# All SBUF tiles of a hybrid decoder step moved by 32 bytes

## Chip, cores and metric

The kernel runs on one core of one Trainium2 chip. The metric is the device time in microseconds (us) of one execution. Before the change it is 1095.63 us, the median of 3 runs (1095.52 to 1095.88).

## What is computed

One inference step of a hybrid decoder layer, in fp32, for a prompt group (512 tokens) and a sample group (8 sequences of 8 tokens). Both share the weights, so the kernel treats them as one block of 576 tokens with 1024 features. Cut to what matters:

```
x = x + post(Wout[concat(Mamba2-SSD heads, mLSTM heads)](pre(x)))   # one combined input projection
x = x + post(CrossAttn(pre(x), memory K/V))
x = x + post((silu(u @ w_gate) * (u @ w_up)) @ w_down),  u = pre(x)  # SwiGLU
```

Every bracket is an RMSNorm, a set of dense projections and some work by head or by token. The projections are nearly all of the work on TensorE.

## The kernel before

**Split products.** A projection is not multiplied in plain fp32. Weights and activations are each split into two fp32r tiles, a rounded copy `hi` and the rest `lo = raw - hi`, and a product is the sum of three matmuls into the same PSUM tile. This is `gemm`, lines 194 to 205, whose three matmuls are lines 201, 202 and 204:

```
mm(ps, wh, ah, start=i == 0, stop=False)
mm(ps, wh, al, start=False, stop=False)
m = mm(ps, tiles[order[c]][1], xh(order[c], t0, n), start=False, stop=c == len(tiles) - 1)
```

`wh` and the third matmul's weight are 128x128 blocks of tiles `whi` and `wlo`; they are the stationary operand, which TensorE loads first (rows PEld). `ah` and `al` are the moving operand, 256, 320 or 288 tokens wide (`HALVES` and `EHALVES`, lines 29 and 32). Lines 1848 to 1850 are the same three matmuls in the feed-forward part, and line 814 those of the mLSTM values, 512 columns wide, where the weights are the moving operand and the activations the stationary one. In all, 6,976 matmuls have fp32r operands: 2,176 with 256 columns, 2,784 with 288, 1,696 with 320, 288 with 512 and 32 with 258.

**Where the parts come from.** `split_w` (line 171) loads 512 KB of weights into a tile `raw`, ScalarE (ACT) casts it to `whi` (line 179), and VectorE (DVE, line 186) or GpSimd (POOL) subtracts. For some tiles a DMA that adds makes `wlo` instead (line 184). `whi` and `wlo` have three buffers each, `raw` has two. Activations are split in the same way (`split`, line 189).

**Order.** The build runs with a scheduler that places instructions by a simulated timeline; the later stages are recorded in an order written out by hand. Each engine then has one fixed list of instructions, with semaphores between them.

**Memory.** All tiles come from pools. The pools of one kind are stacked upward from the bottom of SBUF: `const` (line 120), `weights` (121), `big` (122, the activation slots `s0`, `s1` and so on), `ml` (278) and the pools that come and go above them. The pools with `side="right"` (lines 680, 940, 1034, 1101, 1380, 2047, 2088) are stacked downward from the top end of SBUF. Inside a pool each tile is rounded up to a multiple of 32 bytes. The pool `const` begins with two long-lived tiles:

```
c32 = cp.tile([P, NLONG], F32, name="c32")
par = cp.tile([P, NPAR], F32, name="par")
```

`c32` has 141 columns (564 bytes a partition, rounded to 576) and `par`, the gains and biases by feature, has 150 (600 bytes, rounded to 608). In the built program `c32` begins at byte 16,512 of a partition, `par` at 17,088, and the next tile at 17,696, which is 276 times 64 plus 32. All tiles behind it have sizes that are multiples of 64 bytes or come in groups that are, so that nearly every operand of a split product begins 32 bytes past a multiple of 64.

Of the kernel before, what the change touches and what calls it, by code (L numbers as in the profile page):

```python
# [11 lines left out]
F32 = mybir.dt.float32  # L12
# [7 lines left out]
P = 128  # L20
# [30 lines left out]
NPAR = _n  # L51
# [64 lines left out]
def build(nc, tc, ctx, I, O):  # L116
    V, A, G, S, TE = nc.vector, nc.scalar, nc.gpsimd, nc.sync, nc.tensor
    mm = TE.matmul

    cp = ctx.enter_context(tc.tile_pool(name="const", bufs=1))  # L120
    wp = ctx.enter_context(tc.tile_pool(name="weights", bufs=1))
    big = ctx.enter_context(tc.tile_pool(name="big", bufs=1))
    pg = ctx.enter_context(tc.tile_pool(name="pg", bufs=3, space=PSUM))
# [25 lines left out]


    c32 = cp.tile([P, NLONG], F32, name="c32")
    par = cp.tile([P, NPAR], F32, name="par")

    def C32(k):
        a, b = _c32[k]
# [144 lines left out]
    psw = MP("ps_warm")  # L300
    for _ in range(NWARM):
        mm(psw[:, 0:256], wz[:, 0:128], wz, start=True, stop=True, skip_group_check=True)
    S.dma_start(par, I["par"])

    wi = [[wp.tile([P, 1024], F32R, name=k, tag=k, bufs=3) for k in ("whi", "wlo")] for _ in range(2)]
    raws = [wp.tile([P, 1024], F32, name="raw", tag="raw", bufs=2) for _ in range(2)]
# [2049 lines left out]
```

## Time and profile before

| what | before |
|---|---|
| median of 3 runs | 1095.63 us |
| span of the profiled execution | 1095.0 us |
| TensorE matmul rows (PE), busy | 1084.1 us, 99% |
| TensorE weight loads (PEld), busy | 1027.5 us, 94% |
| VectorE (DVE) busy | 754.0 us, 69% |
| ScalarE (ACT) busy | 611.7 us, 56% |
| GpSimd (POOL) busy | 225.8 us, 21% |
| mean granted TensorE clock | 0.998 |
| DMA | 182.29 MB, mean 166 GB/s |

The span is that of one profiled execution, from its first instruction to its last; the median of the runs lies 0.6 us above it. The profile gives every instruction a start and a duration. Matmuls overlap each other in the array: a row's duration (0.28 us for 256 columns, say) is longer than the distance from its start to the next one's start (0.12 us). What a matmul costs in a stream is therefore read from the starts in the timeline and not from the durations. L201 is line 201 of the kernel.

### The profile page before, as it was taken

What the parts mean: (1) busy time and instruction counts of PE and PEld (TensorE: products, weight loads), DVE (VectorE), ACT (ScalarE), POOL (GpSimd) and SP (SyncE); (2) the same over time, 40 slices, a digit from 0 to 9 for tenths busy, and PEclk for the clock granted to TensorE, in tenths of its full rate; (3) what the DMA queues carried; (4) which work ended last, traced back from release to release, by engine and by line L of the source; (5) the groups of instructions that cost most, each with busy time, mean ns of one, the idle gap of its engine ahead of it and who ended that gap; (6) DMA issues with size and microseconds to landing.
All of it is one profiled execution on the core that took longest, in us unless ns stands there. A gap on an engine that the chain in (4) does not pass through costs nothing.

```text
span 1095.0 us, 20715 instructions
## 1 busy us (share of the span) xinstructions
PE 1084.1 (99%) x8124; PEld 1027.5 (94%) x8124; DVE 754.0 (69%) x1507; ACT 611.7 (56%) x1098; POOL 225.8 (21%) x305
## 2 busy tenths in 40 slices
PE   9999999999999999999999999999999999999997
PEld 8999887778999999999988879999999999999997
DVE  6896785658877775558744546676566877787555
ACT  7767632455654555656545445645566566656653
POOL 1332643313213112000144301100011121111000
PEclk9999999999999999999999999999999999999999
DMA  6785635435655349653467775644386687588532
GB/s 204 170 154 127 170 111 174 163 84 177 189 149 146 106 132 312 205 189 102 150 215 271 264 248 163 217 161 109 104 195 142 150 196 173 116 188 186 128 130 88
DMA packets 58967, 182.29 MB, mean 166 GB/s; under 512 B 6605, under 2 KB 11853, under 8 KB 58357
## 3 DMA queue, kind: packets, MB, share of 16 engines
q1 hardware_dynamic: 42740, 138.06, 39.0%
q0 software_dynamic: 15552, 41.95, 19.8%
q8 instruction: 64, 1.05, 0.4%
q10 hardware_dynamic: 576, 0.95, 0.3%
q14 instruction: 35, 0.28, 0.1%
HBM read 160.28 MB, written 20.65 MB: 165 GB/s over the span
## 4 chain that ended last, share of the span: by engine, by line
PE 88%; DVE 5%; ACT 4%; DMA 2%; issue 1%; SPq 0%; POOL 0%; DVEq 0%; ACTq 0%
PE ps_v L814 5%; PE ps_in L202 4%; PE ps_in L201 4%; PE ps_in L204 4%; PE ps_o L202 3%; PE ps_o L204 3%; PE ps_o L201 3%; PE ps_g L1848 3%; PE ps_g L1849 3%; PE ps_g L1850 3%; PE ps_u L1848 3%; PE ps_u L1850 3%; PE ps_u L1849 3%; PE ps_dn L1848 2%; PE ps_dn L1849 2%; PE ps_dn L202 2%
## 5 line engine op out<-in xcount | busy, mean ns | idle before, releaser
L201 PE MATMUL ps_in<-uh,whi 128*128 128x320 f32 (+1 forms) x544 | 164.0, 302 | 0.4 <-DVE cb L450 0.4
L204 PE MATMUL ps_in<-uh,wlo 128*128 128x320 f32 (+1 forms) x544 | 163.2, 300 | 0.0
L202 PE MATMUL ps_in<-ul,whi 128*128 128x320 f32 (+1 forms) x544 | 162.7, 299 | 0.0
L179 ACT CAST whi<-raw 128x1024 fp32r<-128x1024 f32 (+1 forms) x104 | 105.2, 1013 | 96.2 <-PE ps_in L202 26.1
L186 DVE TENSOR_TENSOR wlo<-raw,whi 128x512 fp32r<-128x512 f32 (+1 forms) x96 | 96.6, 1009 | 66.5 <-ACT whi L179 65.8
L201 PEld LDWEIGHTS ps_in<-uh,whi 128*128 128x128 f32 x544 | 103.1, 190 | 3.4 <-issue 1.7
L204 PEld LDWEIGHTS ps_in<-uh,wlo 128*128 128x128 f32 x544 | 103.0, 190 | 1.2 <-issue 0.4
L202 PEld LDWEIGHTS ps_in<-ul,whi 128*128 128x128 f32 x544 | 103.1, 190 | 0.6
L184 POOL DMA_DIRECT2D wlo<-win x32 | 27.9, 871 | 80.1 <-ACT wlo L183 72.0
L1848 PE MATMUL ps_g<-b,whi 128*128 128x288 f32 x144 | 42.5, 295 | 0.0
L1849 PE MATMUL ps_g<-b,whi 128*128 128x288 f32 x144 | 42.4, 295 | 0.0
L1848 PE MATMUL ps_u<-b,whi 128*128 128x288 f32 x144 | 42.4, 295 | 0.0
L1849 PE MATMUL ps_u<-b,whi 128*128 128x288 f32 x144 | 42.4, 295 | 0.0
L1821 ACT CAST whi<-rawx 128x1024 fp32r<-128x1024 f32 (+1 forms) x26 | 25.7, 987 | 27.8 <-PE ps_dn L1849 13.8
L191 DVE TENSOR_TENSOR wlo<-sw,whi 128x1024 fp32r<-128x1024 f32 (+1 forms) x26 | 29.6, 1140 | 14.9 <-ACT whi L190 14.7
L201 PE MATMUL ps_xo<-qh,whi 128*128 128x288 f32 x128 | 38.5, 302 | 0.2 <-ACT whi L179 0.2
L202 PE MATMUL ps_o<-mixs_l,whi 128*128 128x320 f32 (+1 forms) x128 | 38.2, 299 | 0.0
L204 PE MATMUL ps_o<-mixm_h,wlo 128*128 128x256 f32 (+1 forms) x128 | 38.2, 298 | 0.0
L202 PE MATMUL ps_o<-mixm_l,whi 128*128 128x256 f32 (+1 forms) x128 | 37.9, 296 | 0.0
L201 PE MATMUL ps_xq<-u2h,whi 128*128 128x320 f32 (+1 forms) x128 | 37.9, 300 | 0.0
L201 PE MATMUL ps_o<-mixm_h,whi 128*128 128x256 f32 (+1 forms) x128 | 37.9, 296 | 0.0
L204 PE MATMUL ps_xq<-u2h,wlo 128*128 128x320 f32 (+1 forms) x128 | 37.9, 296 | 0.0
(765 smaller groups left out, 3838.9 us busy)
## 6 DMA issues: line engine op xcount, KB each, us to landing
raw<-win SPq DMA_DIRECT2D x35, 512.0 KB, 3.9
raw<-wout SPq DMA_DIRECT2D x17, 512.0 KB, 3.6
raw<-wxq SPq DMA_DIRECT2D x13, 512.0 KB, 3.6
raw<-wgate SPq DMA_DIRECT2D x13, 512.0 KB, 3.5
raw<-wup SPq DMA_DIRECT2D x13, 512.0 KB, 5.3
wlo<-win POOLq DMA_DIRECT2D x24, 256.0 KB, 5.1
kva<-kc SPq DMA_DIRECT2D x12, 512.0 KB, 5.7
kva<-vc SPq DMA_DIRECT2D x12, 512.0 KB, 6.0
```

Of the source, the lines that this page charges most:

```text
L179: casts.append(A.copy(hi[:, :n], raw[:, :n]))
L184: G.dma_start(lo[:, a:b], src[:, a:b], accum_op=ALU.add)
L186: e.tensor_tensor(lo[:, a:b], raw[:, a:b], hi[:, a:b].bitcast(F32), op=ALU.subtract)
L191: (eng or V).tensor_tensor(lo, src, hi.bitcast(F32), op=ALU.subtract)
L201: mm(ps, wh, ah, start=i == 0, stop=False)
L202: mm(ps, wh, al, start=False, stop=False)
L204: m = mm(ps, tiles[order[c]][1], xh(order[c], t0, n), start=False, stop=c == len(tiles) - 1)
L814: mm(ps, a, b, skip_group_check=True, **kw)
L1821: A.copy(s.h3[:, s.all], s.r2[:, s.all])
L1848: mm(ps, wh, b[0][k], start=start and k == 0, stop=False, skip_group_check=True)
L1849: mm(ps, wh, b[1][k], start=False, stop=False, skip_group_check=True)
L1850: m = mm(ps, wl, b[0][k], start=False, stop=k == nk - 1, skip_group_check=True)
```

## The change

```
+    edge = ctx.enter_context(tc.tile_pool(name="edge", bufs=1, side="right"))
+    edge.tile([P, 8], F32, name="edge")
...
-    par = cp.tile([P, NPAR], F32, name="par")
+    par = cp.tile([P, 160], F32, name="par")
...
-    S.dma_start(par, I["par"])
+    S.dma_start(par[:, 0:NPAR], I["par"])
```

`par` becomes 640 bytes a partition in place of 608, so the tile behind it begins at 17,728, which is 277 times 64, and everything that is stacked upward lies 32 bytes higher than before. The tile `edge` (8 columns, 32 bytes) is never read or written; it takes the topmost 32 bytes, so everything that is stacked downward lies 32 bytes lower. `par` is filled by the same DMA with the same 150 columns. Nothing else is different. Instruction for instruction, the lists of all five engines are the same in the two built programs, with the same semaphores; only the addresses are others. 957 tiles lie 32 bytes higher, 153 lie 32 bytes lower.

Of the 6,976 fp32r matmuls, 6,944 had both operands at 32 past a multiple of 64, and have both at a multiple of 64 now. The other 32 (line 987) had their stationary operand at a multiple of 64 and have it at 32 past now.

Two relations change or stay, beside the plain position. Between two tiles of the same stack the distance is as before. Between a tile of the lower stack and one of the upper stack it changes by 64 bytes. Take the moving operand of a matmul and the stationary operand of the next one, which is loaded while the first one streams: in 5,434 such pairs the two stood a multiple of 128 bytes apart, and still do; in 1,275 they stood 64 bytes off a multiple of 128, and now are a multiple of 128 apart.

## The prediction

> **What bounds the kernel now.** The page comes first: busy shares, the granted clock, and the chain that ended last.
>
> ```profile
> span 1095.0 us, 20715 instructions
> PE 1084.1 (99%) x8124; PEld 1027.5 (94%) x8124; DVE 754.0 (69%) x1507; ACT 611.7 (56%) x1098; POOL 225.8 (21%) x305
> PEclk9999999999999999999999999999999999999999
> PE 88%; DVE 5%; ACT 4%; DMA 2%; issue 1%; SPq 0%; POOL 0%; DVEq 0%; ACTq 0%
> ```
>
> TensorE holds 88% of the chain, at full clock throughout. The list of waits shows nearly nothing that it waits for; these are its two longest:
>
> ```profile
> PE ps_warm L302 <- DVE wz L299: 1.1, 1, 1.1
> PE ps_ss L227 <- DVE ssqx L268: 0.8, 1, 0.8
> ```
>
> Where is the chain not on TensorE? In the first 112 us, by the chain for that window alone:
>
> ```profile
> by line: DVE ac L462 13.7%; issue 9.0%; DMA xraw<-xT 8.2%; DMA raw<-win 7.5%; ACT whi L179 6.5%; DVE cb L450 5.3%; ACT ac L460 5.2%; DVE pl L500 5.1%; DVE ssqx L268 3.4%; DVE wlo L186 2.8%; ACT wlo L183 2.6%; ACT L464 2.3%; DVE mrw L520 1.2
> ```
>
> DVE, ACT and the first loads set the pace there. Behind that, TensorE does. The table by stage (length, then busy us and instructions of PE, PEld, DVE, ACT, POOL, then clock, DMA share and GB/s) shows the room that the others have:
>
> ```profile
> 60.00:112.00 52.00, 51.15 (x374) 49.26 (x374) 41.39 (x76) 38.84 (x64) 17.82 (x44) 1.00 0.70 137
> 112.00:270.00 158.00, 157.83 (x1068) 129.45 (x1068) 108.78 (x205) 69.64 (x112) 61.35 (x67) 1.00 0.50 149
> 270.00:390.00 120.00, 120.00 (x895) 114.23 (x894) 94.44 (x262) 62.64 (x136) 24.72 (x31) 1.00 0.50 143
> 700.00:1087.00 387.00, 386.83 (x2918) 385.36 (x2918) 272.68 (x508) 227.24 (x389) 47.97 (x57) 1.00 0.62 148
> ```
>
> DVE is busy 69% (108.78 of 158), 79% (94.44 of 120) and 70% (272.68 of 387) of these stages. So the time behind 112 us is the number of matmuls times what one costs in a stream, and the change can only act through that cost.
>
> **What a matmul costs in a stream.** The durations overlap, so I take distances between starts. First and last of four undisturbed streams in the timeline, with 18, 18, 15 and 9 matmuls from the first start to the last (256, 320, 288 and 512 columns):
>
> ```profile
> 446.73 0.28 PE L201 MATMUL ps_o<-mixm_h,whi 128*128 128x256 f32 x1
> ...
> 448.89 0.28 PE L201 MATMUL ps_o<-mixm_h,whi 128*128 128x256 f32 x1
> ```
> ```profile
> 450.05 0.31 PE L201 MATMUL ps_o<-mixm_h,whi 128*128 128x320 f32 x1
> ...
> 452.69 0.31 PE L201 MATMUL ps_o<-mixm_h,whi 128*128 128x320 f32 x1
> ```
> ```profile
> 743.88 0.29 PE L201 MATMUL ps_g<-u3h,whi 128*128 128x288 f32 x1
> ...
> 745.88 0.30 PE L201 MATMUL ps_g<-u3h,whi 128*128 128x288 f32 x1
> ```
> ```profile
> 223.91 0.39 PE L814 MATMUL ps_v<-whi,uh 128*128 128x512 f32 x1
> ...
> 225.95 0.39 PE L814 MATMUL ps_v<-whi,uh 128*128 128x512 f32 x1
> ```
>
> That is 2.16 / 18 = 120.0 ns, 2.64 / 18 = 146.7, 2.00 / 15 = 133.3 and 2.04 / 9 = 226.7. From 256 to 320 columns the cost grows by 26.7 ns, 0.417 ns a column; from 320 to 512 by 80.0 ns, again 0.417. So every fp32r matmul costs its columns times 0.417 ns **plus 13.3 ns**, the time of 32 columns, whatever its width. All these operands start at 32 past a multiple of 64. The 6,976 matmuls have 857 us of columns in them (2,176 x 256 + 2,784 x 288 + 1,696 x 320 + 288 x 512 + 32 x 258 = 2,057,000 columns), and the 13.3 ns make another 93 us. Those 93 us are what the change can touch.
>
> Plain fp32 transposes, 128 columns wide, show a smaller remainder:
>
> ```profile
> 1084.17 0.87 PE ps_ft L2190 x8
> ```
>
> 0.87 / 8 = 109 ns each; read as 128 columns at half the fp32r rate (106.7 ns), that leaves 2.1 ns. It bounds the gain: at most 13.3 - 2.1 = 11.2 ns a matmul could go. It bounds it in another way too. Each of them loads a 128-column weight, and 109 ns is as close as such loads are seen to follow each other, so a 256-column matmul could not fall below about 109 from 120.0.
>
> **Does the 13.3 ns hang on addresses?** One place says that it does in part. The groups by form of the output projection, whose two halves differ only in the tiles that stream (busy us, mean ns of one):
>
> ```profile
> L204 PE MATMUL ps_o<-mixs_h,wlo 128*128 128x256 f32 x64 | 17.9, 279 | 0.0
> L201 PE MATMUL ps_o<-mixs_h,whi 128*128 128x256 f32 x64 | 17.9, 280 | 0.0
> L202 PE MATMUL ps_o<-mixs_l,whi 128*128 128x256 f32 x64 | 18.2, 285 | 0.0
> ...
> L204 PE MATMUL ps_o<-mixm_h,wlo 128*128 128x256 f32 x64 | 18.3, 286 | 0.0
> L202 PE MATMUL ps_o<-mixm_l,whi 128*128 128x256 f32 x64 | 18.1, 283 | 0.0
> L201 PE MATMUL ps_o<-mixm_h,whi 128*128 128x256 f32 x64 | 18.1, 283 | 0.0
> ```
>
> Three matmuls of `mixs` take 279 + 280 + 285 = 844 ns, three of `mixm` 852: 2.7 ns less for one, close to 8 columns or **32 bytes of a streamed row** (3.33 ns). `mixs_h` lies in the upper stack, 64 bytes off the weights' position modulo 128; `mixm` lies in the lower one, in step with them. So an address relation is worth about one such step.
>
> **The change, part by part.**
> - *Instructions.* None is added, removed or moved on any engine, no wait is added, and the DMA of `par` brings the same bytes. Cost nothing.
> - *TensorE's operands.* 6,944 matmuls go from 32 past a multiple of 64 to a multiple of 64. If rows are fetched in pieces of 64 bytes, such a row now begins and ends within a piece: a 256-column row takes 17 pieces now and 16 then. No row of the trace shows an fp32r stream whose two operands start at a multiple of 64. The bounds are 0 and 11.2 ns a matmul, from the remainders above. I take one step of 32 bytes, **3.33 ns**, because the only row pair in which addresses alone differ moved by 2.7 ns. It is an estimate.
> - *What of it reaches the end.* 722 of the matmuls start before 112 us, where the chain is DVE, ACT and loads: nothing is taken for them. 6,254 start later: 6,254 x 3.33 ns = 20.8 us. The 270 to 390 us stage, with DVE at 79%, will give some back when TensorE asks for its tiles earlier; I take off 1 us. If that cover were gone altogether, its share, 895 of the 8,124 matmul records, would be 2.3 us.
> - *The other engines.* DVE shows both positions. Line 757 works at multiples of 64 throughout, line 1811 at 32 past:
>
> ```profile
> L757 DVE TENSOR_TENSOR h<-h,ps_hu 128x512 f32<-128x512 f32 x16 | 10.6, 680 | 7.0 <-PE ps_hu L756 6.0 <-issue 1.0
> L1811 DVE TENSOR_TENSOR rawx<-raw,rawx 128x512 f32<-128x512 f32 x18 | 12.3, 684 | 0.0
> ```
>
>   680 against 684 ns, with PSUM in the one and not in the other: nothing that would count, and it lies beside TensorE anyway. I take nothing, between -0.6% and +0.6% of DVE's part of the chain (5% of 1095), 0.3 us either way.
> - *DMA.* Every transfer lands 32 bytes off its old place. On the chain it counts only at the start:
>
> ```profile
> 0.74 3.89 DMA xraw<-xT
> 6.44 5.25 DMA xraw<-xT
> 11.70 4.97 DMA raw<-win
> ```
>
>   14.1 us in all; rows 3.89 and 5.25 are the same transfer of two slices, so half their spread, 0.7 us, bounds it either way. I take nothing.
>
> Sum: 20.8 - 1 = 19.8 us off the profiled execution's 1095.0, 1075.2; the runs' median lies 0.6 above the span, so **1075.8 us**.
>
> The Trainium skill speaks against a gain: "SBUF — State Buffer", section "Specifications (TRN2)", puts SBUF's cachelines at 16 bytes, and 32 past a multiple of 64 is as much a multiple of 16 as 64 is. By that rule nothing changes and the sum would be 1095.6; the 2.7 ns between `mixs` and `mixm` is not explained by 16-byte lines, so this trace does not settle it. "TensorE: Matmul & The Clock Gate", section "Wait — 56ns, not 53.3ns?", has a warm bf16 matmul at its columns plus about 2.5 ns; this trace's fp32r streams show 13.3, so by that page some 10.8 ns would be left to gain.
>
> **The rivals.**
> - *A whole piece goes, not half of one.* If the extra 64-byte piece costs its full 16 columns, each matmul loses 6.67 ns: 6,254 x 6.67 = 41.7, less some 2 us of waits that come back in front of DVE, so 1056 us. For it: the remainder is exactly 32 columns in four widths, so it looks made of whole pieces. Against it: nothing in the trace falls by 16 columns.
> - *Nothing.* The 13.3 ns belong to fp32r itself, and addresses that are multiples of 16 or 32 are all alike: 1095.6. For it: the remainder is the same at every width, and DVE does not notice the position. Against it: `mixs`.
> - *Slower: the two stacks fall into step.* In 1,275 pairs a streaming operand stood 64 bytes off the next weights' position modulo 128, as `mixs_h` does, and the change brings them into step, like `mixm`. Each loses its step: 1,275 x 3.33 = 4.2 us, 1099.8 (with the measured 2.7 ns, 3.4 us, 1099.0). It decides if the plain position gains less than 4.2 us / 6,254 = 0.68 ns a matmul. For it: the pair of groups above. Against it: in 320 columns `mixs` and `mixm` are alike, so not every pair has something to lose.
> - *The change does not do what it says.* The built program's addresses exclude it: 6,944 of 6,976 matmuls are at multiples of 64 afterwards.
>
> **How the numbers follow.** One step: 0.33. A whole piece or more: 0.27. Nothing: 0.19. In step and slower: 0.21. The likeliest gives 1075.8. The forecast's own range is 1068 to 1085. The range for 8 in 10 reaches from below the whole-piece case, 1048, to just above the slower case, 1100; it leaves out some 0.06 below (the full 11.2 ns would be 70 us, 1025) and some 0.1 above. About 0.2%, 2.2 us, can be told from no change in this kernel. Faster by more: the two gaining cases, 0.60. Within: 0.18, most of "nothing". Slower by more: 0.22.
>
> **What would show it.** In the profile after, the four streams would read 116.7, 143.3, 130.0 and 223.3 ns from start to start; 113.3, 140.0, 126.7 and 220.0 for a whole piece; unchanged for nothing. For the slower case the `mixs` groups rise to those of `mixm` and those of `mixm` stay. PE's waits on DVE between 270 and 390 us would grow by about 1 us. The prediction is wrong if the four streams keep their 13.3 ns, or if they lose it and the end stays, in which case another engine has taken over.

## The result, and the profile after

The change makes no difference that can be told: 1096.64 us after it (median of 13 runs, 1095.95 to 1097.63) against 1096.15 before (13 runs, 1095.08 to 1097.01). The ratio is 1.0006, 95% interval 0.9998 to 1.0014. The forecast was 1075.8.

The page after, the lines that answer to those of before (span, busy time by engine, granted clock, chain):

```profile
span 1094.7 us, 20715 instructions
PE 1084.4 (99%) x8124; PEld 1028.0 (94%) x8124; DVE 753.0 (69%) x1507; ACT 611.4 (56%) x1098; POOL 226.0 (21%) x305
PEclk9999999999999999999999999999999999999999
PE 86%; DVE 5%; ACT 4%; issue 2%; DMA 2%; POOL 0%; SPq 0%; DVEq 0%; ACTq 0%; POOLq 0%
```

TensorE still holds the chain at full clock. So nothing was gained and then lost elsewhere: had a matmul become cheaper and TensorE waited for others, PE would have fewer busy us. The table by stage says the same (length, then busy us and instructions of PE, PEld, DVE, ACT, POOL, then clock, DMA share, GB/s):

```profile
270.00:390.00 120.00, 120.00 (x897) 114.44 (x896) 94.41 (x263) 62.34 (x136) 24.65 (x31) 1.00 0.51 144
700.00:1087.00 387.00, 386.79 (x2919) 385.36 (x2917) 272.57 (x507) 226.75 (x389) 47.88 (x57) 1.00 0.61 148
```

897 matmuls are counted from 270 to 390 us where 895 were, and 2,919 from 700 to 1087 us where 2,918 were. The list of TensorE's waits is empty for both stretches, before and after.

The four streams that the prediction named as its test, first and last matmul of each in the timeline (start, duration; line 203 is line 201 of before, line 816 is line 814), with 21, 15, 21 and 9 matmuls between the two starts:

```profile
446.37 0.28 PE L203 MATMUL ps_o<-mixm_h,whi 128*128 128x256 f32 x1
...
448.89 0.28 PE L203 MATMUL ps_o<-mixm_h,whi 128*128 128x256 f32 x1
...
450.13 0.31 PE L203 MATMUL ps_o<-mixm_h,whi 128*128 128x320 f32 x1
...
452.33 0.31 PE L203 MATMUL ps_o<-mixm_h,whi 128*128 128x320 f32 x1
...
743.18 0.29 PE L203 MATMUL ps_g<-u3h,whi 128*128 128x288 f32 x1
...
745.98 0.29 PE L203 MATMUL ps_g<-u3h,whi 128*128 128x288 f32 x1
```
```profile
222.90 0.39 PE L816 MATMUL ps_v<-whi,uh 128*128 128x512 f32 x1
...
224.94 0.39 PE L816 MATMUL ps_v<-whi,uh 128*128 128x512 f32 x1
```

2.52 / 21 = 120.0 ns, 2.20 / 15 = 146.7, 2.80 / 21 = 133.3, 2.04 / 9 = 226.7: each as before. All these operands now begin at a multiple of 64 bytes, and the 13.3 ns beyond the columns stand.

One thing did move. The groups by form of the output projection (busy us, mean ns of one):

```profile
L203 PE MATMUL ps_o<-mixs_h,whi 128*128 128x256 f32 x64 | 18.2, 284 | 0.0
L204 PE MATMUL ps_o<-mixs_l,whi 128*128 128x256 f32 x64 | 18.1, 283 | 0.0
L206 PE MATMUL ps_o<-mixs_h,wlo 128*128 128x256 f32 x64 | 18.1, 283 | 0.0
```
```profile
L206 PE MATMUL ps_o<-mixm_h,wlo 128*128 128x256 f32 x64 | 18.3, 286 | 0.0
L204 PE MATMUL ps_o<-mixm_l,whi 128*128 128x256 f32 x64 | 18.1, 283 | 0.0
L203 PE MATMUL ps_o<-mixm_h,whi 128*128 128x256 f32 x64 | 18.1, 283 | 0.0
```

Three matmuls of `mixs` went from 844 to 850 ns; those of `mixm` stayed at 852. The advantage of `mixs` is gone. It was not an advantage of position, which both have in common; it belonged to the 64 bytes between the two stacks, which the change takes away.

To see all of it, every start of one trace is set against the same start of the other, and the pairs are grouped by what the built programs' addresses say: the width of the matmul, and the distance, modulo 128 bytes, by which the start of its moving operand lies past the start of the next matmul's stationary operand. I call this the **distance** from here on. Mean ns from start to start, undisturbed pairs only:

```
columns  distance before -> after   pairs   before   after
256        0 -> 0                    1632   119.73   119.62
256       64 -> 0                     341   117.41   119.75
288        0 -> 0                    2148   132.40   132.35
288       64 -> 0                     598   132.47   132.60
320        0 -> 0                    1322   147.09   146.83
320       64 -> 0                     287   145.85   146.63
512        0 -> 0                     235   230.07   230.39
```

Where the distance is kept, the intervals change by -0.1 to -0.3 ns up to 320 columns and by +0.3 at 512 (the next kernel shows the same changes without a new position). Where the 64 bytes go, 256 columns lose 2.3 ns, 320 lose 0.8 and 288 nothing. All pairs together sum to +0.5 us. The medians differ by as much (1096.64 - 1096.15), though by no more than their scatter.

The profiled execution of after is 0.3 us shorter in its span, not longer. Its first loads on the chain were quicker by more than the pairs lost:

```profile
0.74 3.60 DMA xraw<-xT
6.15 4.56 DMA xraw<-xT
10.73 4.69 DMA raw<-win
```

12.9 us where that of before had 14.1. Such loads scatter between executions: in the kernels below, the second of them took between 4.66 and 5.31 us, and the three together 13.3 to 13.6.

### The profile page after: what moved, and what is told of

Its sections match the earlier page's. It is cut to its first block, busy times and chain, and to the rows that moved or that the text cites. A ratio compares the mean times of both kernels' runs of the same rounds, so it can differ in the third digit from the quotient of the medians.

```text
span 1094.7 us, 20715 instructions
## 1 busy us (share of the span) xinstructions
PE 1084.4 (99%) x8124; PEld 1028.0 (94%) x8124; DVE 753.0 (69%) x1507; ACT 611.4 (56%) x1098; POOL 226.0 (21%) x305
## 4 chain that ended last, share of the span: by engine, by line
PE 86%; DVE 5%; ACT 4%; issue 2%; DMA 2%; POOL 0%; SPq 0%; DVEq 0%; ACTq 0%; POOLq 0%
PE ps_in L204 4%; PE ps_in L203 4%; PE ps_in L206 4%; PE ps_v L816 3%; PE ps_o L206 3%; PE ps_o L203 3%; PE ps_o L204 3%; PE ps_g L1850 3%; PE ps_g L1851 3%; PE ps_g L1852 3%; PE ps_u L1850 3%; PE ps_u L1852 3%; PE ps_u L1851 3%; PE ps_dn L1850 2%; PE ps_dn L1851 2%
## 5 line engine op out<-in xcount | busy, mean ns | idle before, releaser
L203 PE MATMUL ps_o<-mixs_h,whi 128*128 128x320 f32 (+1 forms) x128 | 38.0, 297 | 0.0
L206 PE MATMUL ps_o<-mixs_h,wlo 128*128 128x320 f32 (+1 forms) x128 | 37.9, 296 | 0.0
```

## The experiments

At this point there were two readings. **Theory A**: the plain position is worth nothing, and only the distance counts, a little. **Theory B**: the position does give something, and the lost distance takes it back.

### Losing the distance without moving the position

```
+    edge = ctx.enter_context(tc.tile_pool(name="edge", bufs=1, side="right"))
+    edge.tile([P, 16], F32, name="edge")
```

This is the kernel before with a tile of 64 bytes at the top end: the upper stack goes down by 64 bytes. Every operand stays at 32 past a multiple of 64, and the distances become those of after.

> Only the upper stack moves, down by 64 bytes; every operand keeps its start at 32 past a multiple of 64, but the 1,275 pairs that were 64 bytes off modulo 128 fall into step, as in the changed kernel. Theory A (the plain position costs and gains nothing, only the relation between the two operands counts): the streams of mixs rise from 25 to 27 columns of remainder to 32 as in the changed kernel, about +1 us, so the time is that of the changed kernel within 0.1%. Theory B (the plain position gained something and the lost relation ate it): the gain is missing here, so it is slower than the changed kernel by what the position gained.

Measured: 1096.43 us (11 runs, 1095.61 to 1097.62) against 1096.11 for before; ratio 1.0002 (0.9993 to 1.0011). The groups of `mixs` are those of after, 850 ns for three:

```profile
L203 PE MATMUL ps_o<-mixs_h,whi 128*128 128x256 f32 x64 | 18.2, 284 | 0.0
L206 PE MATMUL ps_o<-mixs_h,wlo 128*128 128x256 f32 x64 | 18.1, 283 | 0.0
L204 PE MATMUL ps_o<-mixs_l,whi 128*128 128x256 f32 x64 | 18.1, 283 | 0.0
```

The table of pairs is that of after almost to the digit: 256 columns at 64 -> 0 rise to 119.78 ns (after: 119.75), 0 -> 0 stays at 119.60 (119.62), 320 columns 146.80 (146.83), and the sum is +0.50 us (+0.51). With or without the 32 bytes the kernel is the same. Theory A holds, and B falls: there is no gain of position for the lost distance to take back.

### More pairs with the distance

```
     wp = ctx.enter_context(tc.tile_pool(name="weights", bufs=1))
+    gap = ctx.enter_context(tc.tile_pool(name="gap", bufs=1))
+    gap.tile([P, 16], F32, name="gap")
     big = ctx.enter_context(tc.tile_pool(name="big", bufs=1))
```

64 bytes between the weights and the activations of the lower stack: now 5,575 pairs stand 64 bytes off, in place of 1,310, all operands still at 32 past a multiple of 64. If it is the distance that counts, `mixm` and all the others should gain what `mixs` had. If it is something of those tiles alone (**theory C**), they should not.

> An unused tile of 64 bytes between the weights' pool and everything above it; every operand keeps its start at 32 past a multiple of 64, but 5,575 pairs in place of 1,310 stand 64 bytes off modulo 128. Theory A: the 256-column streams of the lower stack fall from 120.0 to about 117.5 ns and the 320-column ones from 147.1 to 145.8; 1,531 x 2.3 ns + 1,245 x 1.25 ns = 5.1 us less, about 1091 us, 0.46% faster. Theory C (the short remainder of mixs belongs to those tiles and not to the relation): no change, 1096 us.

Measured: 1093.46 us (11 runs, 1091.77 to 1095.57) against 1096.11; ratio 0.9977 (0.9969 to 0.9986). The page's first line and the stream of `mixm` at 256 columns, first and last of 9 intervals:

```profile
span 1090.6 us, 20715 instructions
```
```profile
445.95 0.28 PE L203 MATMUL ps_o<-mixm_h,whi 128*128 128x256 f32 x1
...
447.01 0.28 PE L203 MATMUL ps_o<-mixm_h,whi 128*128 128x256 f32 x1
```

1.06 / 9 = 117.8 ns, where it was 120.0. In the table of pairs:

```
columns  distance before -> here    pairs   before    here
256        0 -> 64                   1613   119.60   117.05
288        0 -> 64                   1442   132.57   132.16
320        0 -> 64                   1287   147.02   146.63
512        0 -> 64                    190   229.93   233.05
```

256 columns gain 2.5 ns (1,613 pairs, -4.1 us), the others little, 512 lose 3. The sum is -4.2 us, and the span of the profiled execution fell by 4.4; the medians differ by 2.7 only, and where the rest goes stays open. The forecast of 5.1 us was too high, mainly because 320 columns gained 0.4 ns where 1.25 was expected. C falls: the distance works in any tiles, but to any extent in one width only.

### The cost of a matmul by itself

A kernel without the layer: streams of 24 matmuls, two stationary blocks in turn, nothing else running, so that the 13.3 ns are seen without other engines.

```
+        def stream(name, n, m, s1, s2, count=24, dt=None, bank="a"):
+            o = ps.tile([P, 512], F32, name=name, tag=bank)
+            for c in range(count):
...
+                st = (s1, s2)[c % 2]
+                mm(o[:, 0:n], w[:, st:st + 128], x[:, m:m + n], start=c == 0, stop=c == count - 1, skip_group_check=True)
```

> Leaves the layer out: only streams of 24 matmuls on otherwise idle engines, with the operands' starts chosen, and zeros as outputs. Theory A: 256 columns cost the same at every common start (0, 4, 8, 16, 32, 64, 96 bytes past a multiple of 128), about 120 ns, and about 117.5 ns where the moving operand alone is moved by 64 modulo 128. Theory B: 120 ns at a start of 32, and about 113 to 117 at 0 and 64. If the 13.3 ns come from other engines' traffic to the memory, all streams here show less. The bf16 stream tells whether the remainder belongs to fp32r: 107 + 13 ns if it does not.

In the timeline each stream is one row (start, duration); from a row's start to the next row's are 24 matmuls. First all operands displaced together: by 0 bytes (`m_pos_a`), 4 (`m_pos_b`), 8 (`m_pos_c`), 16 (`m_pos_d`), 32 (`m_pos_e`), 64 (`m_pos_f`) and 96 (`m_pos_g`):

```profile
35.33 3.03 PE L142 MATMUL m_pos_a<-X,W 128*128 128x256 f32 x24
38.20 3.09 PE L142 MATMUL m_pos_b<-X,W 128*128 128x256 f32 x24
41.13 3.04 PE L142 MATMUL m_pos_c<-X,W 128*128 128x256 f32 x24
44.01 3.00 PE L142 MATMUL m_pos_d<-X,W 128*128 128x256 f32 x24
46.85 3.02 PE L142 MATMUL m_pos_e<-X,W 128*128 128x256 f32 x24
49.71 3.03 PE L142 MATMUL m_pos_f<-X,W 128*128 128x256 f32 x24
52.58 3.03 PE L142 MATMUL m_pos_g<-X,W 128*128 128x256 f32 x24
...
78.15 2.88 PE L142 MATMUL m_mov_i<-X,W 128*128 128x256 f32 x24
80.87 3.00 PE L142 MATMUL m_mov_j<-X,W 128*128 128x256 f32 x24
...
177.54 2.79 PE L142 MATMUL m_bf_a<-XB 128*128 128x256 bf16 x24
180.17 5.34 PE L142 MATMUL m_bf_b<-XB 128*128 128x512 bf16 x24
185.35 5.34 PE L142 MATMUL m_fp_a<-raw 128*128 128x256 f32 x24
190.53 5.34 PE L142 MATMUL m_fp_b<-raw 128*128 128x256 f32 x24
```

At 0, 32 and 64 bytes 24 matmuls take 2.87, 2.86 and 2.87 us: 119.6, 119.2 and 119.6 ns. **Between 32 past a multiple of 64 and a multiple of 64, position is worth nothing in the barest case too.** Theory A had forecast about 120 ns at every common start, and two came out otherwise: 4 bytes took 2.93 us, 122.1 ns, and 16 bytes 2.84 us, 118.3 ns. Then the moving operand alone displaced: 112 bytes (`m_mov_i`) take 2.72 / 24 = 113.3 ns, 6.7 less, with the mean of the intervals inside at 117.9 for 64 bytes, 113.3 for 16 and 114.1 for 192. At 288 and 320 columns 64 bytes change nothing (131.4 and 146.7 either way, behind the first two intervals). Streams of 64 to 192 columns ran partly at a granted clock of 0.5 and aren't used.

The last rows show what the 13.3 ns belong to. bf16 with 256 columns takes 2.63 / 24 = 109.6 ns, with 512 5.18 / 24 = 215.8: 512 columns by 0.417 are 213.3, so 2.5 ns remain. Each row of the plain fp32 streams, 256 columns at half the rate, takes 215.8 as well, with the moving operand displaced by 32 bytes or not (a plain fp32 matmul has two such rows: the 24 here are 12 matmuls). Only fp32r carries 13.3 ns, and it does so on an otherwise idle chip.

### The kernel's order of three

In those streams the moving operand never changed. **Theory D** says that 113.3 ns comes from that; the kernel's order of `gemm` changes it all the time. Again the layer is left out: 24 matmuls in the kernel's order, over 8 blocks, with the moving operand displaced in steps of 16 bytes.

```
+            for k in range(8):
...
+                for c, (i, j) in enumerate(((0, 0), (0, 1), (1, 0))):
+                    st, mv = (xs[j], ws[i]) if wide else (ws[i], xs[j])
+                    mm(o[:, 0:n], st, mv, start=k == 0 and c == 0, stop=k == 7 and c == 2, skip_group_check=True)
```

> Leaves the layer out: on idle engines, streams with the kernel's own order of three matmuls (hi x hi, hi x lo, lo x hi) over 8 blocks, in its widths (256 columns from token 0, 320 from token 256, 288 from 0 and from 288, and 512 with the weights moving). The moving operand is displaced by 0, 16, 32 up to 256 bytes against the stationary one, and once both are displaced by 32 bytes. Theory A: the common displacement changes nothing in any width; the displacement between the two changes 256 columns as in the streams before (113.3 ns at 16 and at 112 bytes modulo 128, about 117.5 at 64, 120 at 0), and the wider ones too where their remainder is made by the same collision. Rival D (the short remainder at 16 bytes came from that stream's unchanging moving operand): no displacement falls below 117 ns at 256 columns.

First and last block of the stream with both operands 32 bytes further on (`n_a_both`) and of that without (`n_a_a`), 21 matmuls apart:

```profile
40.48 0.28 PE L146 MATMUL n_a_both<-XH,WH 128*128 128x256 f32 x1
...
42.99 0.28 PE L146 MATMUL n_a_both<-XH,WH 128*128 128x256 f32 x1
43.35 0.28 PE L146 MATMUL n_a_a<-XH,WH 128*128 128x256 f32 x1
...
45.85 0.28 PE L146 MATMUL n_a_a<-XH,WH 128*128 128x256 f32 x1
```

2.51 against 2.50 us: the change of this case, made alone, is nothing in this order too. By displacement of the moving operand, and behind the first six intervals, 256 columns gave 119.7 ns at 0, 118.5 at 16, 116.9 at 32, 117.7 at 64, 119.8 at 80, 113.3 at 112 and at 192, 120.0 at 256. So D, which had nothing below 117, falls: 112 and 192 bytes still give 113.3. Only at 16 bytes is the 113.3 gone. 320 columns stay near 146.7 nearly everywhere (153.4 at 208), 288 columns lie between 130.1 and 135.5, and 512 are best at 0 (226.7; 229 to 234 elsewhere).

### Three quarters of 256 bytes, in the layer

192 bytes looked better than 64, so the two lower pools change places with a gap between them, and the upper stack moves by 64 bytes; in 4,400 pairs the moving operand then begins 192 bytes past the next weights, modulo 256. The first kernel is made from before (all operands at 32 past a multiple of 64), the second from after (all at multiples of 64):

```
-    wp = ctx.enter_context(tc.tile_pool(name="weights", bufs=1))
...
     big = ctx.enter_context(tc.tile_pool(name="big", bufs=1))
+    gap = ctx.enter_context(tc.tile_pool(name="gap", bufs=1))
+    gap.tile([P, 16], F32, name="gap")
+    wp = ctx.enter_context(tc.tile_pool(name="weights", bufs=1))
```

> The pools weights and big change places, an unused 64-byte tile stands between them and one at the top end: every operand still starts at 32 past a multiple of 64, but 4,400 pairs stand 192 bytes off modulo 256, 1,629 of them with 256 columns. Theory A, with the idle streams' numbers (113.3 ns at 192, 119.7 at 0, 117.7 at 64): 256-column matmuls fall to about 113.4 ns, 1,629 x 5.9 ns = 9.6 us less; 320 and 288 columns unchanged; 512 columns + 2 ns x 214 = 0.4 us. About 1087 us, 0.8% faster than the kernel before. Rival E (only the distance modulo 128 counts, so 192 is like 64): about 117.3 ns at 256 columns and 3 to 4 us less, 1092.5 us.

> The same exchange of pools and the same unused 64-byte tile in the changed kernel: every distance between operands is as in the run before it, but every operand starts at a multiple of 64. Theory A: the same time as the run before it within 0.1%, and the same streams. Theory B (the plain position counts, and the lost relation hid it): faster than the run before it by what the position gains.

Measured, against 1095.79 for before: 1093.11 us (9 runs, 1092.61 to 1094.83), ratio 0.9979 (0.997 to 0.9989), and 1092.78 us (7 runs, 1091.98 to 1093.69), ratio 0.997 (0.9959 to 0.9981). The two are twins in every row of the table: 256 columns at 0 -> 192 fall from 119.79 to 116.46 in the one and to 116.42 in the other, 288 columns at 0 -> 192 rise from 131.93 to 133.05 and 133.02, and the sums over all pairs are -4.3 and -4.5 us. This is the second pair of kernels that differ in position alone, and again it counts for nothing. The second kernel is the best of the study, 0.3% under before.

It should have been better. The expected 113.4 ns came out as 116.4, and the expected 1087 us as 1093.11; the forecast's rival E, by which 192 bytes are no more than 64, was nearer with 1092.5. But it isn't that each matmul took 116.4: of 1,588 intervals in the first kernel 29% were at or under 115 ns and 69% between 116 and 119, in the same tiles. Two explanations were left: what the other engines do meanwhile, and what TensorE itself runs.

### Do the other engines cost it?

**Theory E** (not the rival E above): what DVE, ACT, POOL and DMA read and write in SBUF meanwhile slows the fast ones. The layer is left out; the streams of three at 0, 16, 64 and 192 bytes are repeated in six phases.

```
+        for phase in ("idle", "dve", "act", "pool", "dma", "all"):
...
+            for k in range(3):
+                for r, x0 in (("zero", 0), ("s", 4), ("h", 16), ("m", 48)):
+                    last = stream(f"{phase}_{r}", 256, 0, x0, 0, "abcdef"[(4 * k + "zshm".index(r[0])) % 6])
```

> The layer is left out: streams of 24 fp32r matmuls of 256 columns in the kernel's order of three, with the moving operand displaced by 0, 16, 64 and 192 bytes against the next weights, three times each, in six phases: the other engines idle, VectorE busy, ScalarE busy, GpSimd busy, 512 KB loads by DMA, and all of these at once. What is open: the exchange of the two pools gave 116.4 ns at 192 bytes where the idle chip gave 113.3. Theory E (what other engines read and write in SBUF meanwhile costs the short relations their advantage): idle 119.7, 118.5, 117.7 and 113.3 ns; with all at once the 192-byte streams rise to 116 or more and the 0-byte streams stay at 119.5 to 120.5; one of the single phases shows which engine it is. Theory F (it lies in the layer's own lists of matmuls, not in traffic): all six phases are alike within 0.3 ns at every displacement. If traffic also lengthened the 0-byte streams, to over 121 ns, the 13.3 ns of remainder would not be fp32r's alone in the kernel.

Two stretches of equal length, out of the idle phase and out of the one with everything at once:

```profile
41.00:74.00 33.00, 33.00 (x281) 33.00 (x280) 0.00 (x0) 0.00 (x0) 0.00 (x0) 1.00 0.00 1
226.00:259.00 33.00, 33.00 (x281) 33.00 (x280) 31.11 (x35) 29.35 (x48) 25.34 (x24) 1.00 0.93 360
```

281 matmuls in both, though in the second DVE is busy 94% and DMA moves 360 GB/s. By displacement: 119.77, 119.00, 117.74 and 117.61 ns idle, and 119.80, 119.00, 117.78 and 117.61 with all at once. The traffic of others does not touch these streams, and theory F holds. But none of them ran at 113.3, so this run alone can't say whether traffic ends that pace: 192 bytes gave 117.6 even idle, where the streams of the kernel's order had 113.3, with the same operands at the same addresses. What differs on TensorE is that the stream at 192 bytes came behind one at 176 there, and behind one at 64 here. (The two also ran on different chips; the next section has both paces in one run.)

The trace of the first kernel with the exchanged pools settles it. Three of its streams at 192 bytes, from the first start to the last, with 23, 23 and 47 intervals (length, then busy us of PE, PEld, DVE, ACT, POOL, then clock, DMA share, GB/s):

```profile
50.73:53.34 2.61, 2.61 (x26) 2.61 (x24) 2.54 (x6) 2.60 (x4) 1.42 (x5) 1.00 0.44 56
434.48:437.18 2.70, 2.70 (x25) 2.70 (x24) 0.00 (x1) 0.43 (x1) 1.06 (x2) 1.00 0.87 261
601.30:606.64 5.34, 5.34 (x49) 5.34 (x48) 4.02 (x12) 3.07 (x10) 1.77 (x1) 1.00 0.82 263
```

The first took 2.61 / 23 = 113.5 ns an interval with DVE and ACT busy nearly throughout, the third 5.34 / 47 = 113.6 with the DMA engines 82% busy; the second took 117.4 with DVE idle and DMA at 87%. **E falls**: streams keep the quick pace beside heavy traffic, and the slow one with DVE idle.

### What ran before

Layer left out, all other engines idle: streams at 192, 112 and 64 bytes, each behind a stream with another displacement.

```
+        for t, x1 in (("m", 48), ("i", 28), ("h", 16)):
+            for p, x0 in (("zero", 0), ("b", 4), ("c", 8), ("e", 16), ("g", 24), ("i", 32), ("l", 44), ("p", 60)):
+                stream(f"pre_{t}_{p}", 256, 0, x0, 0, "abcdef"[k % 6])
+                last = stream(f"then_{t}_{p}", 256, 0, x1, 0, "abcdef"[(k + 1) % 6])
```

> The layer is left out: streams of 24 fp32r matmuls of 256 columns in the kernel's order of three, all other engines idle. Each stream with the moving operand displaced by 192, 112 or 64 bytes against the next weights comes right behind a stream with another displacement (0, 16, 32, 64, 96, 128, 176 or 240 bytes). What is open: with the same addresses, 192 bytes gave 113.0 ns behind a stream of 176 bytes and 117.6 ns behind one of 64 bytes, with the other engines busy or idle alike. Theory G (the short relations have more than one steady pace, and what ran before decides which one a stream falls into): 192 bytes gives 113 to 114 ns behind some displacements, 176 among them, and 117 to 118 behind others, 64 among them, each pace held through its stream; 64 bytes gives 117 to 118 behind all. Theory H (the pace is a matter of the addresses alone, and the two runs differed in something else): 192 bytes gives one pace, within 0.5 ns, behind all eight.

First and last block, 21 matmuls apart: 192 bytes behind 16 (`then_m_b`) and behind 64 (`then_m_e`), then 64 bytes behind 0 (`then_h_zero`) and behind 16 (`then_h_b`):

```profile
48.65 0.28 PE L146 MATMUL then_m_b<-XH,WH 128*128 128x256 f32 x1
...
51.12 0.28 PE L146 MATMUL then_m_b<-XH,WH 128*128 128x256 f32 x1
...
59.84 0.28 PE L146 MATMUL then_m_e<-XH,WH 128*128 128x256 f32 x1
...
62.22 0.28 PE L146 MATMUL then_m_e<-XH,WH 128*128 128x256 f32 x1
...
132.66 0.28 PE L146 MATMUL then_h_zero<-XH,WH 128*128 128x256 f32 x1
...
135.13 0.28 PE L146 MATMUL then_h_zero<-XH,WH 128*128 128x256 f32 x1
...
138.29 0.28 PE L146 MATMUL then_h_b<-XH,WH 128*128 128x256 f32 x1
...
140.67 0.28 PE L146 MATMUL then_h_b<-XH,WH 128*128 128x256 f32 x1
```

2.47 / 21 = 117.6 ns, 2.38 / 21 = 113.3, 117.6, 113.3. With the same addresses a stream keeps one of **two paces**. In this run 192 bytes fell to 113.3 behind six of the eight and stayed at 117.8 behind 16 and 128 bytes; 64 bytes fell to 113.3 behind three (16, 32 and 64 itself, once reached) and stayed at 117.8 behind the other five; 112 bytes ended at 113.3 behind all eight, behind some of them only after ten matmuls or more. The PSUM bank of the output, which changes from stream to stream too, does not sort them: 64 bytes took 117.8 and 113.3 in each of the three banks used. H falls, and theory G holds in its main part: two paces, and a choice that hangs on what ran before. Its details were wrong: 192 bytes behind 64 was forecast at 117 to 118 and gave 113.3, and 64 bytes was forecast at one pace.

Nor is the stream right before all of it. 192 bytes behind 64 kept 117.6 in all repeats of the run with traffic and fell to 113.3 here, though the 64-byte stream ahead kept 117.8 both times; 64 bytes behind 16 kept 117.7 there and ran at 113.3 here. So something further back counts as well, or the chip, which was another one; these runs do not tell which. A stream at a distance of 0 settled at 120.0 in every run here.

The layer has the same two paces. In the first kernel with the exchanged pools there are 47 stretches of at least 16 undisturbed intervals in a row at 192 bytes. The last nine intervals of each average 113.2 to 113.4 ns in 15 of them and 116.9 to 117.9 in 32. What picks the pace there was not tried by itself.

## Why the prediction was wrong, step by step

- **What bounds the kernel: right.** TensorE sets the end behind 112 us, and other engines have room. The kernels that did lower the cost of a matmul got it back in the end, if not in full: 4.2 us in the pairs of the 64-byte gap were 4.4 in the span of the profiled execution and 2.7 between the medians.
- **What a matmul costs: right for the streams it read.** Columns by 0.417 ns plus 13.3 ns held there in after, and on an idle chip at 256, 320 and 512 columns. It is not the cost of every fp32r matmul, as the text had it: over all undisturbed pairs that stood in step, before has 132.4 ns at 288 columns and 230.1 at 512, and the pairs 64 bytes off have 117.4 at 256.
- **TensorE's operands: the step that failed.** The prediction put it as "I take one step of 32 bytes, 3.33 ns, because the only row pair in which addresses alone differ moved by 2.7 ns". The row pair was read rightly, 844 against 852 ns, and even its cause was named, the 64 bytes between the stacks. But it was then used as the price of something else, the position of an operand by itself, which `mixs` and `mixm` have in common. A difference between two rows can price only what differs between them. The position measured next to nothing in every pair of twins: 119.62 ns in after against 119.60 with the edge alone, 116.42 against 116.46 in the exchanged pools, 2.51 against 2.50 us for 21 matmuls in the kernel's order, 119.6 against 119.2 ns in the barest stream. 6,254 x 3.33 ns = 20.8 us was therefore 6,254 x 0.
- **The bounds.** The upper bound of 11.2 ns was taken from plain fp32 transposes, with the thought that what fp32r has beyond them might hang on addresses. The bf16 and fp32 streams confirm the remainder, 2.5 ns, but in those types: fp32r has its 13.3 ns at either position.
- **The 1 us of waits given back** between 270 and 390 us had nothing to follow from; TensorE has no listed wait there before or after.
- **DVE and DMA: right as far as they can be seen.** Of the loads at the start, one execution differs from another by more than the 0.7 us that I allowed: 1.2 us here. Nothing ties that to the change: the three loads took 13.3, 13.4 and 13.6 us in kernels whose lower stack starts at 32 past a multiple of 64, and 13.4 in the one other kernel where it starts at a multiple of 64.
- **The 0.6 us from span to median** set one execution's span against other executions. An execution's own time lies 1.8 us above its span (1096.49 and 1094.7 in the profiled one of after).
- **The rival "nothing"** is what happened, to within the scatter, and its chance was put at 0.19. What spoke against it in the text was `mixs`, the same misplaced evidence. The Trainium skill, "SBUF — State Buffer", section "Specifications (TRN2)", with its lines of 16 bytes had it right for the step of this change: 32 and 64 bytes are alike in all runs. The barest streams don't bear the rule out in full. A common displacement of 4 bytes cost 122.2 ns for 120.0 and one of 8 bytes 120.0, but one of 16 bytes, which should be like 0, gave 118.3, each in one stream whose pace may also hang on what ran before. The distance, on which the same operands take 113.3 to 120.0 ns at multiples of 16, is not in that rule.
- **The rival "slower: the two stacks fall into step"** had the mechanism. Its sign was seen just as named: `mixs` rose to `mixm`, and `mixm` stayed. Only its size was off: 1,275 pairs were each given 3.33 ns, 4.2 us. Only the pairs of 256 columns have 2.3 ns to lose (341 pairs, 0.8 us), those of 320 have 0.8 (287 pairs, 0.2 us), those of 288 nothing. With small gains in the pairs that kept their distance the sum is 0.5 us.
- **The rival "a whole piece"** fell with the forecast.

## What to carry to other kernels

When two rows differ in their time, list everything in which they differ, and price with them only that: here a relation between two operands was booked as a property of one. Before an alignment is forecast for thousands of instructions, look for rows that have it and rows that have not, with all else alike; where the trace has none, the position has no price, and no change is the forecast to start from. In fp32r products that alternate weights, where the streaming operand lies against the next weights can be worth 0.2 to 0.3% of a kernel bound by TensorE, at no cost in instructions, but it has to be measured in the kernel's own order.

## What the runs showed of the hardware that was not expected

- An fp32r matmul with 128x128 weights that change each time settles at its columns by 0.417 ns plus 13.3 ns, at 256, 320 and 512 columns (120.0, 146.7 and 226.7 ns), when its moving operand and the next weights are a multiple of 256 bytes apart; 288 columns took 131.4 to 131.6 ns there, 11.5 beyond their columns. A row of bf16 or plain fp32 has 2.5 ns.
- At 256 columns and some other distances (64, 112 and 192 bytes), part of the 13.3 ns goes: 117.7 or 113.3 ns in place of 120.0. The same addresses have both paces, and which of them a stream keeps hangs on more than the stream right before it.
- The Trainium skill, "TensorE: Matmul & The Clock Gate", section "Step-by-step: what each phase is for", has the weights read through a port of their own, so that loading the next ones takes nothing from the running stream. That the pace of fp32r hangs on the distance between the two operands suggests that here they are not quite independent. Why, these runs do not show; nor whether the next weights count or the matmul's own, since in nearly all of these streams both lie alike modulo 256.
- Other engines' traffic (DVE 94% busy, ACT 89%, POOL 77%, 360 GB/s of DMA) changed fp32r streams of 256 columns by 0.04 ns at most, at paces of 117.6 to 120.0 ns; in the layer the pace of 113.3 stood beside a DVE and an ACT that were busy nearly throughout.
